# Gate and up of layer 1 by seven block products instead of eight

## The chip, the cores and the metric
The kernel runs on one core of one Trainium2 chip. The metric is the device time of one execution in microseconds (us), the median of several runs. The engines are TensorE (PE; its weight loads are PEld), VectorE (DVE), ScalarE (ACT), GpSimd (POOL) and SyncE (SP), whose queue issues the DMAs.

## The reference
A decoder trunk of two layers on 512 tokens of 1024 features, all in float32. Each layer is a mixer (attention) and a SwiGLU feed-forward block, each behind a modulated RMSNorm; the hidden width is 2816. Cut to what matters here:

```python
D_MODEL = 1024
SEQ = 512
DEPTH = 2
FFN_HIDDEN = ((8 * D_MODEL // 3 + 255) // 256) * 256

def _swiglu(h, wg, wu, wd):
    return (jax.nn.silu(h @ wg) * (h @ wu)) @ wd

def reference(x, c, ...):
    cond = jax.nn.silu(c)
    for l in range(DEPTH):
        mod = cond @ ada_w[l] + ada_b[l]
        sh1, sc1, g1, sh2, sc2, g2 = [m[:, None, :] for m in jnp.split(mod, 6, axis=-1)]
        h = _rms_norm(x, norm_mix[l]) * (1.0 + sc1) + sh1
        ...
        x = x + g1 * (y @ w_out[l])
        h = _rms_norm(x, norm_ffn[l]) * (1.0 + sc2) + sh2
        x = x + g2 * _swiglu(h, ffn_gate[l], ffn_up[l], ffn_down[l])
    return x
```

## The kernel before
**Arithmetic.** Activations lie feature-major: x is eight tiles (k-tiles) of 128 features by 512 tokens. A float32 product is made of three products of rounded operands: every operand is split into hi (a copy rounded to float32r, on ScalarE) and lo (the operand less hi, on VectorE), and `mm3` (line 438) issues hi x hi, hi x lo and lo x hi, each a matmul with a weight load of its own. `mms` (line 422) issues them all on line 431.

**Weights.** `stream` (line 519) lists units of 128 partitions x 2048 columns, one DMA of 1 MB each on SP, into `raw` (three slots). `prep_to` (line 546) splits a unit in four pieces of 512: four copies (`whi`, on ScalarE, `copy`/`act`, line 457) and four subtractions (`wlo`, `tt`, line 473, on VectorE; in an early part of layer 0 the second half of a unit on GpSimd). `whi` and `wlo` have three slots each, and a slot comes free when the whole unit has been used. `unit` (line 561) hands out the next unit and records the splits of those ahead.

**Gate and up.** Each layer has 22 tiles f of 128 hidden features. One unit `wg` holds the gate and the up weights of one f: 2 x 8 blocks of 128 x 128, the gate's in the first 1024 columns. `ffn_tile` (line 1100) makes 8 k-tiles x 2 results x 3 = 48 matmuls of 512 tokens into two PSUM banks, then Silu (ScalarE), the product (VectorE), a rounded copy (ScalarE) and the remainder (VectorE) into `hid`. The first two f run in two halves of 256 tokens (96 matmuls of 256 columns each), so that they can begin when the norm of the first half is done. `ffn` (line 1113) does f = 0 to 10, then a down product over these (`reduce_out`, line 1071), then f = 11 to 21 and the last down product.

**Order.** Nothing runs in the order of the text. Each operation is recorded with an estimated duration (`mm_ns`, `ve_ns`, the sums in `act`) and with the tiles it touches; a list scheduler (`once`, line 240) then simulates the engines, lets each take the ready operation of the smallest number first (VectorE's are renumbered by when TensorE would want the result, `due`, line 216), gives out the slots of `raw`, `whi`, `wlo`, `t2` (61 tiles of 512 columns: activations, `hid`, temporaries), `sm` and `ps` (eight PSUM banks), and writes a fixed order for each engine. The waits between engines follow from the tiles. A tag can have a cap (`gu`, the banks of gate and up: 4), and t2 keeps 8 tiles for whoever is next in the recorded order.

Names in the trace: `t` is any t2 tile, `ps` a PSUM bank, `raw`, `whi`, `wlo` the weights, `x` the residual.

Of the kernel before, what the change touches and what calls it, by code (L numbers as in the profile page):

```python
# [17 lines left out]
P = 128  # L18
# [7 lines left out]
BIG = 1e30  # L26
TOPK = 128
# [50 lines left out]
class View:  # L78
# [32 lines left out]
    def region(self):  # L111
        """bits of the (32-partition quadrant, column block) pairs touched, and elements per partition"""
# [46 lines left out]
class Sched:  # L159
    CROSS, SAME, DMA = 270, 130, 2300  # L160
    # the PE's clock is halved at first and for a while after a long gap
# [54 lines left out]
    def due(self):  # L216
        """priorities from when the PE, kept busy in the present order, would want each result"""
# [151 lines left out]
class Kern:  # L369
    def __init__(self, ctx, tc, io, out):  # L370
# [887 lines left out]
```

## Time and profile before
| | us |
|---|---|
| median of 3 runs (1207.24 to 1208.63) | 1207.81 |
| span of the profiled execution | 1205.3 |
| TensorE busy | 1180.9 |
| VectorE busy | 707.4 |
| ScalarE busy | 487.1 |
| GpSimd busy | 87.9 |

The span goes from the first to the last instruction of one execution; the runs' median is 2.5 us above it. A busy time is a sum over the whole span and says nothing of which engine sets the time in one stage; for that, look at a stretch alone. The mixer of layer 0 (with its output product) runs to some 300 us, its feed-forward block to some 665, the mixer of layer 1 to some 840; the gate and up tiles of layer 1 from f = 3 on lie from 873 to 960 and from 1020 to 1140 us, each group followed by its down product.

### The profile page before, as it was taken

The page shows a single profiled execution, that of the slowest core. Times are in us where ns is not written, and L with a number is a line of the kernel's source. Part 1 is how long each engine was busy: PE and PEld are TensorE (multiplying, and loading weights), DVE is VectorE, ACT ScalarE, POOL GpSimd, SP SyncE. Part 2 cuts the span into 40 slices and gives each one's busy share as a digit, 9 for nine tenths or more (in the row PEclk, how much of TensorE's full clock was granted, in tenths as well). Part 3 has the DMA queues.
Part 4 walks back from the last instruction along what each step waited for, and adds up shares of the span by engine and source line. Part 5 has one row for each costly group of instructions (what it writes and reads, how often), then busy time and mean ns, then how long its engine had stood idle before and what let it go on. Part 6 is the DMA issues. An engine that isn't in the chain of part 4 may idle for free.

```text
span 1205.3 us, 16639 instructions
## 1 busy us (share of the span) xinstructions
PE 1180.9 (98%) x6424; PEld 956.2 (79%) x6424; DVE 707.4 (59%) x1656; ACT 487.1 (40%) x1194; POOL 87.9 (7%) x224
## 2 busy tenths in 40 slices
PE   6989999999999999999999999999999999999998
PEld 3867667679988888888889876669988888888888
DVE  5599999847875456655443967748633323233321
ACT  5464376755433221232232666755423312223310
POOL 0142332300000000000000120100000000000000
PEclk9999999999999999999999999999999999999999
DMA  9545612202585546655511322011422223322211
GB/s 349 228 140 175 245 41 101 76 31 71 179 299 185 175 155 216 226 189 175 175 59 65 105 71 71 1 71 70 141 105 77 98 88 105 105 105 95 80 53 36
DMA packets 32415, 151.58 MB, mean 126 GB/s; under 512 B 3152, under 2 KB 4304, under 8 KB 21072
## 3 DMA queue, kind: packets, MB, share of 16 engines
q1 hardware_dynamic: 32336, 150.52, 35.6%
q8 instruction: 50, 0.82, 0.3%
q14 instruction: 29, 0.24, 0.1%
HBM read 148.41 MB, written 2.10 MB: 125 GB/s over the span
## 4 chain that ended last, share of the span: by engine, by line
PE 89%; DVE 7%; ACT 2%; issue 1%; POOL 0%; DMA 0%; SPq 0%; DVEq 0%; POOLq 0%; ACTq 0%
PE ps L431 86%; PE ps L442 3%; DVE t L488 2%; ACT t L457 1%; DVE wlo L473 1%; DVE sm L857 1%; DVE t L858 1%; DVE t L473 1%; DVE t L493 1%; DVE t L481 1%; DMA x<-in_x 0%; POOL sm L473 0%; DVE sm L499 0%; ACT whi L457 0%; ACT sm L457 0%
## 5 line engine op out<-in xcount | busy, mean ns | idle before, releaser
L431 PE MATMUL ps<-t,whi 128*128 128x512 f32 (+2 forms) x2864 | 774.7, 358 | 0.9 <-ACT t L457 0.9
L431 PEld LDWEIGHTS ps<-t,whi 128*128 128x128 f32 x2864 | 506.7, 189 | 82.8 <-issue 4.5
L431 PE MATMUL ps<-t,wlo 128*128 128x512 f32 (+2 forms) x1432 | 509.9, 356 | 0.0
L431 PEld LDWEIGHTS ps<-t,wlo 128*128 128x128 f32 x1432 | 270.6, 189 | 38.1
L457 ACT ACTIVATE t<-ps 128x512 f32<-128x512 f32 (+6 forms) x274 | 120.3, 475 | 399.5 <-PE ps L431 372.2
L457 ACT ACTIVATE whi<-raw 128x512 fp32r<-128x512 f32 x364 | 206.8, 621 | 163.3 <-PE ps L431 98.9
L473 DVE TENSOR_TENSOR wlo<-raw,whi 128x512 fp32r<-128x512 f32 x340 | 221.8, 691 | 38.7 <-ACT whi L457 38.3
L473 DVE TENSOR_TENSOR t<-ps,t 128x128 fp32r<-128x128 f32 (+4 forms) x120 | 56.2, 489 | 220.5 <-PE ps L431 202.1
L431 PE MATMUL ps<-whi,t 128*128 128x512 f32 (+1 forms) x512 | 172.9, 394 | 1.1 <-DVE t L488 1.1
L431 PEld LDWEIGHTS ps<-whi,t 128*128 128x128 f32 x512 | 95.0, 189 | 29.5 <-issue 7.8
L488 DVE SCALAR_TENSOR_TENSOR x<-ps,mod,x 128x512 f32<-128x512 f32 (+1 forms) x64 | 39.3, 616 | 115.2 <-PE ps L431 114.7
L431 PE MATMUL ps<-wlo,t 128*128 128x512 f32 (+1 forms) x256 | 96.5, 377 | 0.0
L488 DVE SCALAR_TENSOR_TENSOR t<-raw,cond,t 128x512 f32<-128x512 f32 x112 | 79.1, 761 | 19.5 <-DMA raw<-in_ada 19.5
L431 PE MATMUL ps<-t,t 64*128 64x256 f32 (+5 forms) x592 | 82.8, 347 | 0.2 <-ACT t L457 0.2
L431 PEld LDWEIGHTS ps<-t,t 64*128 64x128 f32 (+2 forms) x592 | 54.3, 181 | 28.4 <-issue 15.1
L457 ACT ACTIVATE t<-t,sm 128x256 f32<-128x256 f32 (+3 forms) x128 | 65.5, 516 | 20.4 <-DVE sm L493 12.6
L442 PE MATMUL ps<-cst,t 128*128 128x128 f32 x388 | 61.8, 279 | 10.0 <-DVE t L473 6.8
L442 PEld LDWEIGHTS ps<-cst,t 128*128 128x128 f32 x388 | 45.0, 140 | 32.6 <-issue 9.9
L481 POOL TENSOR_SCALAR sm<-sm 128x8 f32<-128x8 f32 (+2 forms) x64 | 18.4, 288 | 550.8 <-DVE sm L499 547.4
L473 DVE TENSOR_TENSOR t<-t,t 128x512 fp32r<-128x512 f32 (+3 forms) x85 | 50.2, 593 | 14.1 <-ACT t L457 13.9
L431 PEld LDWEIGHTS ps<-wlo,t 128*128 128x128 f32 x256 | 48.4, 189 | 6.2
L493 DVE CUSTOM_DVE_ANT_0 t<-ps,cst 128x256 f32<-128x256 f32 (+3 forms) x104 | 39.1, 409 | 18.5 <-PE ps L431 18.1
(72 smaller groups left out, 564.6 us busy)
## 6 DMA issues: line engine op xcount, KB each, us to landing
raw<-in_wg SPq DMA_DIRECT2D x44, 1024.0 KB, 4.8
raw<-in_ada SPq DMA_DIRECT2D x40, 1024.0 KB, 5.3
raw<-in_wd SPq DMA_DIRECT2D x20, 1024.0 KB, 4.7
raw<-in_w0c SPq DMA_DIRECT2D x10, 1024.0 KB, 6.1
t<-in_ada SPq DMA_DIRECT2D x32, 256.0 KB, 6.5
raw<-in_wo SPq DMA_DIRECT2D x8, 1024.0 KB, 4.8
raw<-in_w1c SPq DMA_DIRECT2D x6, 1024.0 KB, 4.7
x<-in_x SPq DMA_DIRECT2D x8, 256.0 KB, 5.1
```

The source lines that it names most:

```text
L431: self.nc.tensor.matmul(o.ap(), l.ap(), r.ap(), start=st, stop=sp, skip_group_check=True)
L442: self.s.op("PE", 107, lambda: self.nc.tensor.transpose(out.ap(), src.ap(), self.ident.ap()), [out], [src, self.ident])
L457: self.nc.scalar.activation(out.ap(), src.ap(), func, **kw)
L473: lambda: self.eng(e).tensor_tensor(out.ap(), a.ap(), b.ap(), op=op), [out], [a, b])
L481: self.eng(e).tensor_scalar(out.ap(), a.ap(), val(s1), val(s2), op0=op0, **kw)
L488: lambda: self.nc.vector.scalar_tensor_tensor(out.ap(), a.ap(), val(s), b.ap(), op0=op0, op1=op1),
L493: lambda: self.nc.vector.tensor_tensor_reduce(out.ap(), a.ap(), b.ap(), op0=OP.add, op1=OP.min, scale=scale, scalar=3e38, accum_out=accum. ...
L857: self.s.op("DVE", 65 + 1.05 * n, lambda m8=m8: self.nc.vector.max(m8.ap(), sc.ap()), [m8], [sc])
L858: self.s.op("DVE", 65 + 1.05 * n, lambda m8=m8: self.nc.vector.match_replace(sc.ap(), m8.ap(), sc.ap(), -3e38), [sc], [m8, sc])
```

## The change
In layer 1, from f = 3 on, gate and up of one tile are no longer two results over all eight k-tiles, but a 2 x 2 block product: the blocks of the weights are (gate, up) by (first, last four k-tiles), those of the activations (first, last four k-tiles) by (first, last 256 tokens). It is done with seven block products in place of eight (the scheme of Winograd's variant of Strassen). Each block product is 4 k-tiles x 3 = 12 matmuls of 256 columns, and three PSUM banks are used.

- `prep_seven` makes the weights' operands: it sums blocks of the raw weights (VectorE, over 1024 and 512 columns), and splits seven operands of 512 columns, the pairs at once over 1024.
- `combos` runs once, ahead of f = 3: it adds the shift to the eight kept norm results `hf`, makes four combinations of them for each pair of k-tiles, and splits them.
- `ffn_seven` runs the products, with two copies, an in-place subtraction in PSUM and two more subtractions between and behind them, then Silu, product and split as before.
- The split weights of all units, in both layers, now lie in 13 tiles of 1024 columns (`w`) in place of three `whi` and three `wlo` of 2048; t2 has 59 tiles instead of 61, with a cap of 18 for the tag T; the cap `gu` is 6 instead of 4; the planner's estimate for GpSimd is 2.48 ns an element instead of 2.1. Units that are not taken apart in sevens are split in pieces of 512 as before (the first unit in pieces of at most 512 within halves of 800).

The diff, cut to its core (removed comments and the arguments `e` and `e_`, which no call sets, are left out):

```diff
+NW, NT2 = 13, 59
+SEVEN, DIRECT = (1,), 3
...
-        s.group("whi", pool("whi", 3), 3, 0, None)
-        s.group("wlo", pool("wlo", 3), 3, 0, None)
-        n = 61
-        s.group("t2", pool("t2", n), n, 8, None, L=12, pT=4, qf=3, q=8, nt=10, hid=26, ada0=20)
+        s.group("w", pool("w", NW), NW, 0, None)
+        n = NT2
+        s.group("t2", pool("t2", n), n, 8, None, L=12, pT=4, qf=3, q=8, nt=10, hid=26, ada0=20, T=18)
-        s.group("ps", pool("ps", 8, space=PSUM), 8, 1, None, mm=3, lg=2, tp=2, pv=2, gu=4, st=7)
+        s.group("ps", pool("ps", 8, space=PSUM), 8, 1, None, mm=3, lg=2, tp=2, pv=2, gu=6, st=7)
...
-            return 165 + 2.1 * n
+            return 165 + 2.48 * n
...
+            if self.seven(i):
+                self.prep_seven(i, raw)
+            else:
+                step = 800 if name == "w0s" else 1024
+                for a in range(0, w, step):
+                    m = min(step, w - a)
+                    self.split_w(i, raw[:, a:a + m], m, 512, e if a else "DVE")
...
+    def split_w(self, i, src, n, step, e="DVE"):
+        hi, lo = (self.s.tile("w", "w", (P, 1024), FR)[:, :n] for _ in range(2))
+        for a in range(0, n, step):
+            b = min(a + step, n)
+            self.copy(hi[:, a:b], src[:, a:b])
+            self.tt(lo[:, a:b], src[:, a:b], hi[:, a:b].bitcast(F), OP.subtract, e=e)
+        self.ws[i].append((hi, lo))
+
+    def prep_seven(self, i, raw):
+        q = raw.rearrange("p (q c) -> p q c", q=4)
+        s13 = self.s.tile("w", "w", (P, 1024))
+        s13v = s13.rearrange("p (q c) -> p q c", q=2)
+        two = lambda: [self.s.tile("w", "w", (P, 1024), FR) for _ in range(2)]
+        halves = lambda t: [t[:, a:a + 512] for a in (0, 512)]
+        self.tt(s13v, q[:, 0::3], q[:, 2][:, None].to_broadcast([P, 2, 512]), OP.add)
+        xh, xl = two()
+        self.copy(xh, raw[:, :1024])
+        self.tt(xl, raw[:, :1024], xh.bitcast(F), OP.subtract)
+        self.tt(q[:, 2], s13[:, 512:], q[:, 0], OP.add)
+        sh, sl = two()
+        self.copy(sh, s13)
+        self.tt(sl, s13, sh.bitcast(F), OP.subtract)
+        self.tt(q[:, 1], q[:, 2], q[:, 1], OP.add)
+        th, tl = two()
+        for a in (512, 0):
+            c = slice(a, a + 512)
+            r = raw[:, 512 + a:1024 + a]
+            self.copy(th[:, c], r)
+            self.tt(tl[:, c], r, th[:, c].bitcast(F), OP.subtract)
+        y = self.s.tile("w", "w", (P, 1024), FR)
+        self.copy(y[:, :512], q[:, 3])
+        self.tt(y[:, 512:], q[:, 3], y[:, :512].bitcast(F), OP.subtract)
+        X, S, T = (list(zip(halves(h), halves(l))) for h, l in ((xh, xl), (sh, sl), (th, tl)))
+        self.ws[i] = [X[0], T[1], S[1], X[1], S[0], T[0], tuple(halves(y))]
...
+    def combos(self):
+        c1, c2 = HALVES
+        T = []
+        for k in range(8):
+            t = self.hf[k]
+            self.act(t, t, AF.Identity, bias=self.mod[1][:, 3, k:k + 1])
+        for k in range(4):
+            f, g = self.hf[k], self.hf[k + 4]
+            p, q = self.t2("T"), self.t2("T")
+            self.tt(p[:, c1], f[:, c1], f[:, c2], OP.subtract)
+            self.tt(p[:, c2], g[:, c2], p[:, c1], OP.add)
+            self.tt(q[:, c1], f[:, c2], g[:, c2], OP.subtract)
+            self.tt(q[:, c2], g[:, c1], p[:, c2], OP.subtract)
+            o = []
+            for t in (p, q):
+                hi, lo = self.t2("h", dt=FR), self.t2("h", dt=FR)
+                self.copy(hi, t)
+                self.tt(lo, t, hi.bitcast(F), OP.subtract)
+                o += [(hi[:, c], lo[:, c]) for c in HALVES]
+            T.append(o)
+        return T
+
+    def ffn_seven(self, H, T, w, hid):
+        c1, c2 = HALVES
+        a, b, e = (self.ps("gu")[:, c1] for _ in range(3))
+        B11 = [tuple(t[:, c1] for t in H[k]) for k in range(4)]
+        B21 = [tuple(t[:, c1] for t in H[k]) for k in range(4, 8)]
+        B22 = [tuple(t[:, c2] for t in H[k]) for k in range(4, 8)]
+        T1, T2, T3, T4 = ([T[k][j] for k in range(4)] for j in range(4))
+
+        def product(out, j, B, start=False):
+            for k in range(4):
+                wh, wl = (t[:, k * P:(k + 1) * P] for t in w[j])
+                self.mm3(out, wh, wl, B[k][0], B[k][1], start and k == 0, k == 3)
+        pq, u, sg = (self.t2("sg") for _ in range(3))
+        product(a, 0, B11, True)
+        self.copy(pq[:, c1], a)
+        product(b, 1, T2, True)
+        self.tt(b, b, pq[:, c1], OP.subtract)
+        self.copy(u[:, c1], b)
+        product(e, 2, T1, True)
+        self.copy(pq[:, c2], e)
+        product(a, 3, B21)
+        self.act(sg[:, c1], a, AF.Silu, after=self.lnexp)
+        product(b, 4, T3)
+        self.tt(u[:, c2], b, pq[:, c2], OP.subtract)
+        product(e, 5, B22)
+        self.tt(sg[:, c2], e, u[:, c1], OP.subtract)
+        self.act(sg[:, c2], sg[:, c2], AF.Silu)
+        product(b, 6, T4)
+        self.tt(sg[:, c1], b, sg[:, c1], OP.mult)
+        self.tt(sg[:, c2], u[:, c2], sg[:, c2], OP.mult)
+        self.copy(hid[0], sg)
+        self.tt(hid[1], sg, hid[0].bitcast(F), OP.subtract)
+        return sg
...
-                sg = self.ffn_tile(H, f, c, w(f), hid[f - a])
+                if l not in SEVEN or f < DIRECT:
+                    sg = self.ffn_tile(H, f, c, w(f), hid[f - a])
+                else:
+                    T = T or self.combos()
+                    sg = self.ffn_seven(H, T, w(f), hid[f - a])
```

`norm_tile` keeps its temporary for the second norm of layer 1 in eight T tiles (`hf`) instead of the tag nt. The seven products are called P0 to P6 below, in the order of `ffn_seven`. No load of weights changes.

## Rows read from the trace of the kernel before

**Rows 1.** Page, part 1: the span; busy time, share and instructions of each engine
```profile
span 1205.3 us, 16639 instructions
...
PE 1180.9 (98%) x6424; PEld 956.2 (79%) x6424; DVE 707.4 (59%) x1656; ACT 487.1 (40%) x1194; POOL 87.9 (7%) x224
```

**Rows 2.** Page, part 4: the chain that ended last, shares by engine
```profile
PE 89%; DVE 7%; ACT 2%; issue 1%; POOL 0%; DMA 0%; SPq 0%; DVEq 0%; POOLq 0%; ACTq 0%
```

**Rows 3.** Stretches: length, busy us (instructions) per engine, granted clock, DMA share, GB/s
```profile
core 0: us, PE busy (x) PEld busy (x) DVE busy (x) ACT busy (x) POOL busy (x), PEclk, DMA share, GB/s
30.00:240.00 210.00, 200.40 (x1239) 147.97 (x1241) 187.15 (x499) 119.94 (x343) 61.58 (x142) 1.00 0.40 144
60.00:240.00 180.00, 170.64 (x1011) 123.15 (x1011) 170.83 (x459) 106.72 (x298) 58.10 (x135) 1.00 0.37 129
855.80:873.00 17.20, 17.20 (x106) 15.43 (x105) 7.19 (x15) 6.15 (x14) 0.00 (x0) 1.00 0.54 184
873.00:960.00 87.00, 87.00 (x385) 72.07 (x384) 29.58 (x48) 25.74 (x48) 0.00 (x0) 1.00 0.28 97
1020.00:1140.00 120.00, 120.00 (x532) 99.37 (x531) 40.12 (x65) 34.65 (x65) 0.00 (x0) 1.00 0.30 104
```

**Rows 4.** What TensorE's matmuls waited for, whole span: total us, times, longest
```profile
PE ps L431 <- DVE t L473: 6.9, 2, 6.4
PE ps L442 <- DVE t L473: 6.8, 8, 2.4
```

**Rows 5.** Timeline of TensorE in a whole gate-up tile: start us, us, what
```profile
873.65 0.62 PE L431 MATMUL ps<-t,whi 128*128 128x512 f32 x2
874.10 0.39 PE L431 MATMUL ps<-t,wlo 128*128 128x512 f32 x1
874.33 0.62 PE L431 MATMUL ps<-t,whi 128*128 128x512 f32 x2
```

**Rows 6.** Timeline of TensorE, a half tile with 256 columns
```profile
846.90 0.40 PE L431 MATMUL ps<-t,whi 128*128 128x256 f32 x2
847.14 0.28 PE L431 MATMUL ps<-t,wlo 128*128 128x256 f32 x1
847.26 0.40 PE L431 MATMUL ps<-t,whi 128*128 128x256 f32 x2
```

**Rows 7.** Timeline of ScalarE: Silu of three whole tiles, and one pair of copies
```profile
873.16 0.60 ACT L457 ACTIVATE t<-ps 128x512 f32<-128x512 f32 x1 [7.81 <-PE ps L431]
873.66 1.15 ACT L457 ACTIVATE whi<-raw 128x512 fp32r<-128x512 f32 x2
...
1030.92 0.60 ACT L457 ACTIVATE t<-ps 128x512 f32<-128x512 f32 x1 [8.23 <-PE ps L431]
...
1139.72 0.60 ACT L457 ACTIVATE t<-ps 128x512 f32<-128x512 f32 x1 [7.66 <-PE ps L431]
```

**Rows 8.** Timeline of VectorE: two products of halves, one whole product, one split pair
```profile
855.06 0.75 DVE L473 TENSOR_TENSOR t<-ps,t 128x256 f32<-128x256 f32 x2
...
873.91 0.69 DVE L473 TENSOR_TENSOR t<-ps,t 128x512 f32<-128x512 f32 x1 [7.57 <-PE ps L431]
874.52 1.28 DVE L473 TENSOR_TENSOR wlo<-raw,whi 128x512 fp32r<-128x512 f32 x2
```

**Rows 9.** Groups by line and shape: x, busy us, mean ns, idle before
```profile
L473 DVE TENSOR_TENSOR wlo<-raw,whi 128x512 fp32r<-128x512 f32 x112 | 71.4, 683 | 18.8 <-ACT whi L457 18.8
...
L473 DVE TENSOR_TENSOR t<-ps,t 128x256 f32<-128x256 f32 x8 | 3.1, 418 | 3.9 <-ACT t L457 3.9
```

**Rows 10.** Timeline around 804 us: a ScalarE copy that VectorE's subtraction waits for
```profile
804.05 1.25 ACT L457 ACTIVATE t<-ps 128x128 fp32r<-128x128 f32 x3 [0.36 <-DVE t L473]
804.36 0.69 DVE L473 TENSOR_TENSOR t<-ps,t 128x128 fp32r<-128x128 f32 x3 [0.34 <-ACT t L457]
```

**Rows 11.** Groups of VectorE by line and shape, 855.8 to 873 us
```profile
L473 DVE TENSOR_TENSOR wlo<-raw,whi 128x512 fp32r<-128x512 f32 x8 | 5.1, 687 | 0.1
```

More of the change, by code (lines that the diff above doesn't have):

```diff
@@ L550, in prep_to @@
             w = self.units[i][2]
+            name, idx, _ = self.units[i]
             raw = self.raws.pop(i)
-            hi = self.s.tile("whi", "whi", (P, 2048), FR)
-            lo = self.s.tile("wlo", "wlo", (P, 2048), FR)
-            for a in range(0, w, 512):
-                b = min(a + 512, w)
-                self.copy(hi[:, a:b], raw[:, a:b])
-                self.tt(lo[:, a:b], raw[:, a:b], hi[:, a:b].bitcast(F), OP.subtract, e="POOL" if a >= 1024 and 2 < i < 15 else "DVE")
-            self.ws[i] = (hi, lo)
@@ L559, in prep_to, with seven @@
-            self.prepped += 1
+            self.ws[i] = []
+            e = "POOL" if 2 < i < 15 else "DVE"
+            if self.seven(i):
[5 more added lines that the diff above has]
+                    self.split_w(i, raw[:, a:a + m], m, 512, e if a else "DVE")
+            self.prepped += 1
+    def seven(self, i):
+        name, idx, _ = self.units[i]
+        return name[:2] == "wg" and int(name[2]) in SEVEN and idx >= DIRECT
@@ L568, in chunk @@
     def chunk(self):
-        ua, ub = self.unit(), self.unit(2)
-        a, b = ([t.rearrange("p (k c) -> p k c", k=4) for t in u] for u in (ua, ub))
-        return lambda k: (a[0][:, k], a[1][:, k]) if k < 4 else (b[0][:, k - 4], b[1][:, k - 4])
+        ts = self.unit() + self.unit(2)
+        return lambda k: tuple(t[:, (k % 2) * 512:(k % 2) * 512 + 512] for t in ts[k // 2])
     def setup(self):
@@ L645, in mod_first, with mod_rest @@
         self.stt(self.G[0][0][:, k:k + 1], self.mod[0][:, 1, k:k + 1], 1.0, self.ng[:, 0, 0, k:k + 1], OP.add, OP.mult)
-    def mod_rest(self, l, v, on_pe):
+    def mod_rest(self, l, v, on_pe, e_="DVE"):
         ps = acc = None
@@ L723, in norm_tile @@
         sh = self.mod[l][:, 3 * n, k:k + 1]
-        t = self.t2("nt")[:, c]
+        if n == 1 and l in SEVEN:
+            if c.start == 0:
+                if k == 0:
+                    self.hf = []
+                self.hf.append(self.t2("T"))
+            t = self.hf[k][:, c]
+        else:
+            t = self.t2("nt")[:, c]
         hi, lo = H[k][0][:, c], H[k][1][:, c]
@@ L951, in even @@
         self.score, self.iw, self.bv = {}, {}, {}
-        hi, lo = self.unit()
-        hi, lo = (t[:, :1600].rearrange("p (k c) -> p k c", k=8) for t in (hi, lo))
-        small = [self.proj_f(H, i, lambda k: (hi[:, k], lo[:, k]), 200, "st") for i in range(NB)]
+        ws = self.unit()
+        w0s = lambda k: tuple(t[:, (k % 4) * 200:(k % 4) * 200 + 200] for t in ws[k // 4])
+        small = [self.proj_f(H, i, w0s, 200, "st") for i in range(NB)]
         w = self.chunk()
@@ L1077, in block @@
             while len(blocks) <= j:
-                hi, lo = self.unit()
+                u = self.unit()
                 w = self.units[self.cursor - 1][2]
-                blocks.extend((hi[:, a:a + P], lo[:, a:a + P]) for a in range(0, w, P))
+                blocks.extend(tuple(t[:, a % 1024:a % 1024 + P] for t in u[a // 1024]) for a in range(0, w, P))
             return blocks[j]
@@ L1104, in ffn_tile @@
             for s in range(2):
-                self.mm3(ps[s][:, c], hi[:, s, k], lo[:, s, k], H[k][0][:, c], H[k][1][:, c], k == 0, k == KT - 1)
+                a = s * 1024 + k * P
+                wh, wl = (t[:, a % 1024:a % 1024 + P] for t in w[a // 1024])
+                self.mm3(ps[s][:, c], wh, wl, H[k][0][:, c], H[k][1][:, c], k == 0, k == KT - 1)
         sg = self.t2("sg")[:, c]
@@ L1119, in w @@
                 if f not in W:
-                    W[f] = [t.rearrange("p (s k c) -> p s k c", s=2, k=8) for t in self.unit()]
+                    W[f] = self.unit()
                 return W[f]
```

13 lines of the change are left out of this document (7 added, 6 removed).

## The prediction
> **What bounds the kernel now.** I read the page's totals first: of a span of 1205.3 us TensorE is busy 1180.9 us (98%), VectorE 707.4 us, ScalarE 487.1 us, GpSimd 87.9 us [rows 1]. A busy TensorE could still be waiting for someone's result, so the chain that ended last comes next: 89% of it lies on TensorE, 7% on VectorE [rows 2]. Shares over the whole span hide stages with other limits, so the third view is the table of stretches [rows 3]. From 60 to 240 us (layer 0's mixer) VectorE is busy 170.8 of 180 us and TensorE 170.6: two engines near their limit. From 873 to 960 us and from 1020 to 1140 us (gate and up of layer 1, from the fourth tile on) TensorE is busy all of the time at a granted clock of 1.00 (the 2.4 GHz level), VectorE 29.6 of 87 and 40.1 of 120 us, ScalarE 25.7 and 34.7. The change is made in these two stretches: only TensorE's work sets their length, and both other engines have two thirds of their time free. Last the waits: the matmuls waited for VectorE 13.7 us in the two largest groups, the longest single wait being 6.4 us [rows 4], none of it in these stretches, where busy time equals length.
>
> **TensorE's part.** A tile's gate and up is now 2 results x 8 k-tiles x 3 products of hi and lo = 48 matmuls of 512 columns. Three of them take 874.33 - 873.65 = 0.68 us from start to start [rows 5], so one takes 0.2267 us and a tile 10.88 us. Counted another way, the Silu at 1030.92 and the one ten tiles later at 1139.72 are 108.80 us apart: 10.88 us again [rows 7]. After the change a tile is 7 products x 4 k-tiles x 3 = 84 matmuls of 256 columns. These exist in the trace, in the half tiles of the first two f: three take 847.26 - 846.90 = 0.36 us [rows 6], 0.120 us each. That is 6.7 ns more than half of 0.2267, and it eats much of the eighth that the seven products save: 84 x 0.120 = 10.08 us. The gain is 0.80 us a tile, and with 19 tiles (f = 3 to 21) 15.2 us, all on the path, for as long as TensorE stays the bound.
>
> The Trainium skill has a rule on this (TensorE: Matmul & The Clock Gate, "Back-to-back issue gap"): at the warm clock a matmul starts N/2.4 + 2.5 ns after the last. By it the two sizes would cost 109.2 and 215.8 ns, an estimate from that page, and the tile would save 1.19 us, 22.5 us in all. The rows stand 11 ns above it at both sizes, and I take the rows.
>
> **VectorE's part in the steady tile.** Here the time could be given back. Back to back, 512 columns cost 874.52 - 873.91 = 0.60 us, and 256 columns, second of a pair that takes 0.75 us with a first of 0.42 us, 0.33 us [rows 8, 9]. So each further 256 cost 0.27 us, and 1024 columns, which the trace does not have, some 1.14 us. prep_seven issues three subtractions or sums of 1024 (s13, xl, sl) and five of 512 (two sums, th's two remainders, y's remainder): 3 x 1.14 + 5 x 0.60 = 6.42 us. ffn_seven issues five of 256 and one of 512 behind the products: 5 x 0.33 + 0.60 = 2.25 us. Together 8.67 us a tile, where now six of 512 make 3.6 us. That is 86% of the new 10.08 us: TensorE stays the bound, but the cover shrinks from 7.3 us to 1.4 us a tile.
>
> What that leaves exposed is bounded from both sides. Below by 0: the order is written out ahead, w holds 13 tiles (7 of the running f, five or six of the next), and P0, P2 and P3 of a tile or P0 of the next can stand where an answer is awaited. Above by the nearest rows for a handover: VectorE idles 0.34 us from a ScalarE copy's start to its own subtraction [rows 10]; five uncovered handovers a tile (xl, sl, th twice, y) would bring it to 8.67 + 1.70 = 10.37 us, 0.29 us over, 5.5 us in all. The new in-place subtraction b - pq makes TensorE wait before the fifth product, with P2 and P3 (2.88 us) between; behind the waiting matmul stand all later ones, but the path (two handovers of 0.34 us, 0.33 us on VectorE, a copy of at most 0.60 us on ScalarE, at most one operation of 1.14 us in front) is 2.75 us. I take 0.1 us a tile, 1.9 us, nearer to 0 because other splits are ready at most handovers.
>
> **ScalarE's part.** Two copies of 1024, three of 512 (a pair of 512 takes 1.15 us [rows 7], so at most 2 x 1.15 + 3 x 0.60 = 4.1 us), three copies and two Silus of 256 and one copy of 512, at most 6 x 0.60 = 3.6 us: 7.7 us, under 10.08. It costs nothing while TensorE and VectorE are slower.
>
> **The start.** combos runs once, between the last norm tiles and the second product of f = 3. VectorE gets 16 operations of 256 and eight of 512: 16 x 0.33 + 8 x 0.60 = 10.1 us; ScalarE 8 Identity and 8 copies, some 10 us. The cover is the stretch from 855.8 to 873 us: 17.2 us in which VectorE works 7.2 us and ScalarE 6.2 us [rows 3]. Of VectorE's, eight splits of two units are 4.8 us [rows 11], in whose place f = 3's 6.42 us comes. So 7.2 - 4.8 + 6.4 + 10.1 = 18.9 us against 17.2: 1.7 us late, which I take. The bounds: 0, as half of the combinations (q) is needed only four products later and P0 and P3 need none; and all of VectorE's 10.1 us plus the eight Identity before it at 0.60, some 15 us, if none of it is covered.
>
> **The rest.** Layer 0 issues the same operations; its weights lie in 13 tiles of 1024 in place of six of 2048, so half a unit comes free earlier, t2 has two slots fewer, gate and up may take six PSUM banks for four, and the planner prices GpSimd at 2.48 ns an element for 2.1. All of this only shifts the written order. In the mixer TensorE idles 210 - 200.4 = 9.6 us after 30 us [rows 3]: no more can be won there, and I let it lose no more than that either; I take 0, and 3 us to each side for the range. DMA issues are the same loads in the same order on SP, and raw still has three slots.
>
> **The sum.** Against the profiled span: 1205.3 - 15.2 + 1.9 + 1.7 = 1193.7 us. The runs' median, 1207.8, lies 2.5 us above that span (what lies around it), so 1196.2 us.
>
> **The rivals.**
> *VectorE takes over, mildly.* Its tile comes to between 10.37 and 10.88 us by handovers and work queued in the wrong order; at 10.6 us the gain is 0.28 x 19 = 5.3 us, less 1.7 at the start: 1204.2. For it: 86% use before any wait. Against: in 60 to 240 us VectorE keeps up 95%.
> *VectorE takes over in full, and the kernel gets slower.* If the new operations, each fed by ScalarE or the one before, do not overlap at their ends, they cost their whole durations, 0.683 us for 512 and 0.418 us for 256 [rows 9], 1.21 us for 1024 by the same step: 3 x 1.21 + 6 x 0.683 + 5 x 0.418 = 9.82 us, and with 1.70 us of handovers 11.5 us a tile. From 10.88 us on the change loses; at 11.5 it loses 0.64 x 19 = 12.2 us and 1.7: 1221.7. Against: six operations a tile, alternately fed by ScalarE, already run 0.60 us apart. This case agrees with a rule of the Trainium skill (VectorE: DVE Perf Modes, "The DRAIN you can't avoid"): the next operation does not start until the pipe is empty. Here it starts 0.08 us before the recorded end.
> *The start is bare.* Up to 15 us of combinations in front of f = 3 cancel the gain: 1207.8 - 15.2 + 1.9 + 13 = 1207.5. Against: P0 and P3, and 10 us free on VectorE ahead of it.
> *The shorter matmul costs only its columns.* With 0.2267 / 2 = 0.1133 us each, a tile is 9.52 us, the gain 25.8 us and the time 1185.6. Against: the 0.120 us of [rows 6] is the same shape in the same kernel, back to back. The rule of TensorE: Matmul & The Clock Gate (the Trainium skill, "Back-to-back issue gap") lies between, at an estimated 1188.9 us by its figures.
> *The written order falls otherwise.* The mixer's 9.6 us move by half, in either direction: 1191.4 or 1201.
>
> **How the numbers follow.** About 0.2% (2.4 us) is what a measurement of this kernel can tell from no change, so faster means under 1205.4 and slower over 1210.2. The forecast has 0.60 (1192 to 1201), the mild takeover 0.12, the full one 0.06, the bare start 0.05, columns alone 0.03, the order 0.07 to each side. Faster: 0.60 + 0.10 + 0.03 + 0.07 + 0.05 = 0.85; same: 0.05 + 0.02 + 0.01 = 0.08; slower: 0.06 + 0.01 = 0.07. The range reaches from 1189 (order gained, both losses at 0) to 1205 (the mild takeover), and leaves out columns alone, the bare start, the full takeover and parts of two others, about 0.18.
>
> **What would show it.** Right: three 256-column matmuls in 0.36 us in the new tiles; tiles 10.1 to 10.3 us apart; VectorE 8 to 9 us busy in each; 1024 columns at about 1.2 us recorded; no TensorE wait over 2 us near the first new tile; the stretch up to the first gate-up tile of layer 1 as long as before, within 3 us. Wrong: a VectorE busy over 95% from f = 3 on with TensorE waiting for it, tiles of 10.6 us or more, a gap of many us ahead of f = 3, or a shift in the mixers larger than the gain.

## The result and the profile after

The median of the changed kernel is 1195.61 us (four executions, 1194.65 to 1198.33), that of the kernel before, on the same chip, 1208.03 us (1207.24 to 1208.63). The ratio is 0.9899, with a 95% interval of 0.9887 to 0.9911: faster by 1.0%. The forecast was 1196.2 us, with a range of 1189 to 1205; it lies 0.6 us above the measured time. The profiled execution has a span of 1194.3 us, 11.0 us less than before; by the medians the gain is 12.4 us. The two differ as executions of one kernel do: the profile of before is of one with a mean granted clock of 1.000, as 6 of the 32 executions of that kernel beside the experiments had (median span 1204.8 us), while the other 26 had 0.997 (1206.2 us) and the changed kernel's four 0.994 to 0.996.

First the page: its totals, and the shares of the chain that ended last.

```profile
span 1194.3 us, 18348 instructions
...
PE 1170.6 (98%) x7108; PEld 979.6 (82%) x7108; DVE 817.6 (68%) x1832; ACT 554.9 (46%) x1305; POOL 84.3 (7%) x224
...
PE 86%; DVE 5%; ACT 1%; POOL 0%; issue 0%
```

Against [rows 1] and [rows 2]: TensorE has more instructions (7108 for 6424) and is busy 10.3 us less; VectorE gained 110.2 us, ScalarE 67.8. TensorE still holds 86% of the chain. These sums don't say where the 11 us lie; the stretches of the changed kernel do. The first is what 855.8 to 873 us was before (up to the Silu of f = 2), the second and third are the new tiles of both halves, the fourth is five tiles.

```profile
core 0: us, PE busy (x) PEld busy (x) DVE busy (x) ACT busy (x) POOL busy (x), PEclk, DMA share, GB/s
859.80:877.00 17.20, 17.20 (x106) 15.42 (x105) 16.06 (x32) 11.08 (x19) 0.00 (x0) 1.00 0.19 62
877.00:958.00 81.00, 81.00 (x668) 80.62 (x667) 72.41 (x117) 50.61 (x97) 0.00 (x0) 1.00 0.34 118
1018.00:1120.00 102.00, 102.00 (x849) 101.81 (x848) 87.12 (x135) 61.36 (x112) 0.00 (x0) 1.00 0.27 94
1050.00:1100.40 50.40, 50.40 (x423) 50.40 (x422) 43.89 (x70) 30.43 (x56) 0.00 (x0) 1.00 0.29 104
```

Where [rows 3] had VectorE at 29.6 of 87 us and 40.1 of 120, it now has 72.41 of 81 and 87.12 of 102, yet TensorE is busy all of the time at a clock of 1.00. In the fourth row five tiles take 43.89 us of VectorE: 8.78 us a tile, with 70 instructions, the 14 that `prep_seven` and `ffn_seven` issue for each. The timeline of VectorE in the changed kernel (start, us, what) gives the length of a tile: the same subtraction, which waits for ScalarE's copy, stands at 1082.17 and 1092.25, 10.08 us apart.

```profile
1082.17 0.43 DVE L475 TENSOR_TENSOR ps<-ps,t 128x256 f32<-128x256 f32 x1 [0.45 <-ACT w L459]
...
1086.37 1.22 DVE L475 TENSOR_TENSOR w<-w 128x1024 fp32r<-128x1024 f32 x1
1087.51 0.68 DVE L475 TENSOR_TENSOR w<-raw,w 128x512 fp32r<-128x512 f32 x1
...
1092.25 0.43 DVE L475 TENSOR_TENSOR ps<-ps,t 128x256 f32<-128x256 f32 x1 [0.45 <-ACT w L459]
```

Its second and third line show what 1024 columns cost: 1087.51 - 1086.37 = 1.14 us to the next start, 1.22 us recorded. The matmuls of the new tiles, as the group of TensorE from 1018 to 1120 us (times, busy us, mean ns):

```profile
L433 PE MATMUL ps<-t,w 128*128 128x256 f32 x847 | 102.0, 283 | 0.0
```

With 84 of them in a tile of 10.08 us it is 0.1200 us from one matmul to the next (the 102.0 us hold two matmuls of 512 columns beside the 847; the mean of 283 ns is that of one from end to end, in a pipeline).

To split the span I use two marks on ScalarE: the Silu of the first whole gate-up tile of layer 0, and that of f = 2 in layer 1, the last before the new tiles. In the changed kernel the second reads:

```profile
877.19 0.60 ACT L459 ACTIVATE t<-ps 128x512 f32<-128x512 f32 x1 [3.45 <-PE ps L433]
```

| | before | after |
|---|---|---|
| Silu of the first whole tile, layer 0 | 330.97 | 333.31 |
| Silu of f = 2, layer 1 | 873.16 [rows 7] | 877.19 |
| from there to the end of the span | 332.1 | 317.1 |

So the new tiles and all behind them are 15.0 us shorter, and what lies ahead of them is 4.0 us longer: 2.3 us up to the first mark, 1.7 us between the marks. 15.0 - 4.0 = 11.0. The gain is where it was forecast; the 4.0 us come from a part of the program in which no arithmetic operation was changed but the combinations and the first weights of f = 3, which came in just ahead of the second mark (without them it is 3.7 us, run 1). What TensorE's matmuls waited for (total us, times, longest) hardly differs from [rows 4]. The one matmul that waits for a remainder of weights is not in the new tiles but at the start of layer 0:

```profile
PE ps L433 <- DVE t L475: 7.1, 3, 6.6
PE ps L444 <- DVE t L475: 7.0, 8, 2.5
...
PE ps L433 <- DVE w L475: 0.4, 1, 0.4
```

```profile
23.57 0.44 PE L433 MATMUL ps<-t,w 128*128 128x384 f32 x1 [0.39 <-DVE w L475]
```

### The profile page after: what moved, and what is told of

Its sections match the earlier page's. It is cut to its first block, busy times and chain, and to the rows that moved or that the text cites. A ratio compares the mean times of both kernels' runs of the same rounds, so it can differ in the third digit from the quotient of the medians.

```text
span 1194.3 us, 18348 instructions
## 1 busy us (share of the span) xinstructions
PE 1170.6 (98%) x7108; PEld 979.6 (82%) x7108; DVE 817.6 (68%) x1832; ACT 554.9 (46%) x1305; POOL 84.3 (7%) x224
## 4 chain that ended last, share of the span: by engine, by line
PE 86%; DVE 5%; ACT 1%; POOL 0%; issue 0%
PE ps L433 82%; PE ps L444 3%; DVE t L910 1%; DVE t L490 1%; DVE sm L909 1%; DVE w L475 1%; ACT t L459 0%; DVE t L475 0%; DVE t L495 0%; POOL sm L475 0%; DVE sm L501 0%; DVE t L483 0%; ACT sm L459 0%; POOL sm L483 0%; DVE sm L490 0%
## 5 line engine op out<-in xcount | busy, mean ns | idle before, releaser
L433 PE MATMUL ps<-t,w 128*128 128x256 f32 (+2 forms) x4980 | 833.7, 328 | 0.9 <-DVE w L475 0.4
L433 PEld LDWEIGHTS ps<-t,w 128*128 128x128 f32 x4980 | 735.4, 190 | 86.0 <-issue 5.3
L475 DVE TENSOR_TENSOR w<-raw,w 128x512 fp32r<-128x512 f32 (+1 forms) x340 | 235.4, 726 | 136.3 <-PE ps L433 105.2
L459 ACT ACTIVATE w<-raw 128x512 fp32r<-128x512 f32 (+1 forms) x364 | 217.1, 645 | 153.8 <-PE ps L433 126.4
L459 ACT ACTIVATE t<-ps 128x256 f32<-128x256 f32 (+6 forms) x331 | 137.9, 447 | 289.7 <-PE ps L433 235.7
L433 PE MATMUL ps<-w,t 128*128 128x512 f32 (+1 forms) x768 | 189.9, 391 | 1.3 <-DVE t L490 1.3
L433 PEld LDWEIGHTS ps<-w,t 128*128 128x128 f32 x768 | 133.6, 190 | 36.7 <-issue 9.3
L490 DVE SCALAR_TENSOR_TENSOR t<-raw,cond,t 128x512 f32<-128x512 f32 x112 | 77.3, 746 | 17.3 <-DMA raw<-in_ada 17.2
L475 DVE TENSOR_TENSOR t<-t,t 128x256 f32<-128x256 f32 (+3 forms) x124 | 66.7, 555 | 20.4 <-ACT t L459 20.2
L475 DVE TENSOR_TENSOR t<-ps,t 128x256 f32<-128x256 f32 (+4 forms) x158 | 66.1, 440 | 19.0 <-ACT t L459 12.7
L459 ACT ACTIVATE t<-t 128x256 f32<-128x256 f32 (+3 forms) x82 | 43.8, 540 | 27.8 <-DVE t L475 27.1
```

The source lines that it names most:

```text
L433: self.nc.tensor.matmul(o.ap(), l.ap(), r.ap(), start=st, stop=sp, skip_group_check=True)
L459: self.nc.scalar.activation(out.ap(), src.ap(), func, **kw)
L475: lambda: self.eng(e).tensor_tensor(out.ap(), a.ap(), b.ap(), op=op), [out], [a, b])
L490: lambda: self.eng(e).scalar_tensor_tensor(out.ap(), a.ap(), val(s), b.ap(), op0=op0, op1=op1),
```

## The experiments

**1. The change without the seven products.** All the rest is kept: 13 tiles of 1024, 59 t2 slots, the bank cap, GpSimd's price (only `hf` goes with the products).

```diff
-SEVEN, DIRECT = (1,), 3
+SEVEN, DIRECT = (), 3
```

> The changed kernel with no tile by seven products; its storage, caps and planner figures stay, and the written order of the mixers is that of the changed kernel. Theory (the seven products give 15.2 us, and some 4 us are lost ahead of them by the new storage and order): 1195.6 + 15.2 = 1210.8 us, 3 us over the kernel before, with the first gate-up tile of layer 1 as late as in the changed kernel. Rival (the seven products give only 11 to 12 us, the delay belongs to them): 1207 to 1208 us.

Measured: 1210.87 us, ratio to before 1.0031 [1.0019, 1.0043]; the marks at 332.70 and 876.84, the tail 332.1 us as before. The seven products alone are worth 1210.87 - 1195.61 = 15.3 us (by the two ratios 0.0132 x 1208 = 15.9). The changes around them cost 3.7 us ahead of f = 3 by the marks, and 0.0031 x 1208 = 3.7 us by the ratio. Up to 841 us each engine has the same instructions in the same order in this trace as in the changed kernel's.

**2. The same tiles with small matmuls only.** From f = 3 on every tile of layer 1 runs in two halves of 256 columns, 96 matmuls without a sum of weights.

```diff
-            if self.seven(i):
+            if False:
...
-                    T = T or self.combos()
-                    sg = self.ffn_seven(H, T, w(f), hid[f - a])
+                    for c in HALVES:
+                        sg = self.ffn_tile(H, f, c, w(f), hid[f - a])
```

> Layer 1's tiles from f = 3 on with eight products in halves of 256 tokens: 96 matmuls of 256 columns a tile, no weight sums, no combinations. Theory (0.120 us a matmul in this stage whatever it belongs to): 11.52 us a tile, 19 x 1.44 = 27.4 us over the changed kernel, 1223.0 us. Rival (a matmul of 256 columns costs half of one of 512, the seven products save an eighth and lose the rest elsewhere): 10.88 us a tile, 1210.8 us.

Measured: 1222.8 us, ratio 1.0129 [1.0115, 1.0142]. On ScalarE's timeline the same half's Silu returns every 11.52 us (1040.70, 1052.22, 1063.74):

```profile
1040.70 0.39 ACT L459 ACTIVATE t<-ps 128x256 f32<-128x256 f32 x1 [4.45 <-PE ps L433]
...
1052.22 0.39 ACT L459 ACTIVATE t<-ps 128x256 f32<-128x256 f32 x1 [4.45 <-PE ps L433]
...
1063.74 0.39 ACT L459 ACTIVATE t<-ps 128x256 f32<-128x256 f32 x1 [4.45 <-PE ps L433]
```

11.52 / 96 = 0.1200 us a matmul, with VectorE's work as small as before. The 0.120 us is the price of the shape, not of waits for VectorE: the rival "columns only" falls by this, and so does any thought that a faster VectorE would shorten the seven products.

**3. One more operation of 1024 on VectorE in each tile.** The sum s13 is made twice, with the same result.

```diff
         self.tt(s13v, q[:, 0::3], q[:, 2][:, None].to_broadcast([P, 2, 512]), OP.add)
+        self.tt(s13v, q[:, 0::3], q[:, 2][:, None].to_broadcast([P, 2, 512]), OP.add)
```

> The first sum over 1024 columns (s13) is made twice for each of the 19 tiles, with the same result: 1.14 us more of VectorE a tile, on the way to the weights. Theory (VectorE works 8.8 us of a tile's 10.08 us, its 1024 columns cost 1.14 us back to back, and the order lets it run ahead): 9.9 us a tile still fit, 1195.6 us, at most 0.2 us a tile (4 us) more. Rival (operations fed by another engine do not overlap, VectorE is at its limit already): 1.14 us x 19 = 22 us more, 1213 to 1217 us.

Measured: 1201.49 us, ratio 0.995 [0.9936, 0.9963]: 5.9 us over the changed kernel, more than the 4 us that my theory allowed and less than the rival's. The tail is 323.6 us, 6.5 more. By busy time alone nothing should be lost: 8.78 + 1.14 = 9.92 us, under 10.08. Three stretches of this kernel show how it is lost all the same:

```profile
1030.00:1110.00 80.00, 80.00 (x669) 80.00 (x668) 75.06 (x110) 46.35 (x86) 0.00 (x0) 1.00 0.30 106
884.00:900.00 16.00, 12.88 (x102) 12.07 (x101) 15.45 (x25) 8.36 (x18) 0.00 (x0) 1.00 0.18 67
1110.00:1130.00 20.00, 18.03 (x148) 17.63 (x147) 19.01 (x34) 12.06 (x26) 0.00 (x0) 1.00 0.26 91
```

From 1030 to 1110 us TensorE is full, as it is in the changed kernel. But 80 us are 7.94 tiles of 10.08 us, 119 VectorE operations at 15 a tile, and VectorE did 110: it falls behind by 8%. The groups of VectorE in these 80 us show with what:

```profile
L475 DVE TENSOR_TENSOR w<-raw 128x1024 f32<-128x1024 f32 x16 | 19.5, 1220 | 0.4 <-PE ps L433 0.2
...
L475 DVE TENSOR_TENSOR t<-ps,t 128x256 f32<-128x256 f32 x21 | 8.5, 419 | 1.1 <-ACT t L459 0.6 <-PE ps L433 0.6
...
L475 DVE TENSOR_TENSOR t<-t,t 128x512 fp32r<-128x512 f32 x4 | 2.7, 685 | 0.0
```

The sums of the weights keep up (16, two for each of eight tiles). What is put off is the end of the tiles' own work: 21 operations from PSUM for 24 in the same stretch of the changed kernel, and 4 remainders of `hid` for 7. That holds TensorE up only later. It loses time behind the start (3.1 us of the 16 from 884 us on) and late in the second group (2.0 of the 20 from 1110), and there it waits for operations on t tiles, of ScalarE and VectorE, not for weights. The timeline of TensorE there (the wait before a start in brackets):

```profile
1121.14 1.70 PE L433 MATMUL ps<-t,w 128*128 128x256 f32 x12 [1.72 <-DVE t L475]
```

The waits of both stretches are 5.1 of the 6.5 us; the rest is not placed. 6.5 us over 19 tiles is 0.34 us a tile: of the 1.14 us added, 0.8 us were taken up. VectorE itself stood idle 4.9 of the 80 us, 0.62 us a tile, though it was behind. So handovers of about this size do exist; in the changed kernel they lie in the 10.08 - 8.78 = 1.3 us that VectorE has left.

**4. Two more.** s13 and xl are both made twice.

```diff
+        self.tt(s13v, q[:, 0::3], q[:, 2][:, None].to_broadcast([P, 2, 512]), OP.add)
...
-        self.tt(xl, raw[:, :1024], xh.bitcast(F), OP.subtract)
+        for _ in range(2):
+            self.tt(xl, raw[:, :1024], xh.bitcast(F), OP.subtract)
```

> The sum s13 and the remainder xl, both over 1024 columns, are made twice: 2.28 us more of VectorE a tile. Theory: 8.8 + 2.3 = 11.1 us a tile, 1.0 us over TensorE's 10.08; VectorE takes over in both groups of tiles, less what it made ahead before the second group: 0.9 to 1.0 us x 19 = 17 to 19 us more, 1212 to 1215 us. Rival (VectorE has more room than its busy time tells): 1196 to 1200 us.

Measured: 1219.49 us, ratio 1.0104 [1.0087, 1.0122], 23.9 us over the changed kernel and past what was expected. The profiled execution was the longest of the four, 1223.41 us, with a span 26.6 us over the changed kernel's: 3.8 us of it lie ahead of f = 3 (the mark stands at 881.00), 22.8 us behind. The 3.8 us are no work of the new tiles: with this edit VectorE's order already differs from 126 us on, in the first mixer. By work alone VectorE's tile is 8.78 + 2 x 1.14 = 11.06 us, 0.98 over TensorE's, 18.6 us in 19 tiles. VectorE is now the bound, busy 76.05 of 78 and 96.78 of 100 us:

```profile
880.00:958.00 78.00, 69.47 (x543) 67.30 (x542) 76.05 (x114) 39.73 (x77) 0.00 (x0) 0.98 0.24 83
1040.00:1140.00 100.00, 93.79 (x748) 92.48 (x747) 96.78 (x141) 54.35 (x100) 0.00 (x0) 0.97 0.27 95
```

TensorE idles 8.5 and 6.2 us here, and its granted clock has come down to 0.98 and 0.97: where it waits again and again, it also works more slowly, by an estimated 0.02 x 78 + 0.03 x 100 = 4.6 us. This is the full takeover of the prediction, and 2.28 us of added work a tile are enough for it.

**5. The 1024 columns in halves.** s13, xl and sl, and the copies that feed them, by 512.

```diff
-        self.tt(xl, raw[:, :1024], xh.bitcast(F), OP.subtract)
+        for c in (slice(0, 512), slice(512, 1024)):
+            self.copy(xh[:, c], raw[:, c])
+            self.tt(xl[:, c], raw[:, c], xh[:, c].bitcast(F), OP.subtract)
```

(the same for s13 with sh and sl)

> The weight operands of the seven products by operations of 512 columns only: s13, xl, sl and the two copies in two halves each. Theory (a wide operation saves 2 x 0.60 - 1.14 = 0.06 us on VectorE and less than 0.1 us on ScalarE): 0.2 us a tile, 9.0 of 10.08 us, hidden: 1195 to 1197 us. Rival (VectorE has no room left at the ends of the two groups, as when s13 is made twice): 2 to 5 us more, 1198 to 1201 us.

Measured: 1196.81 us, ratio 0.9905 [0.9891, 0.992], not to be told from the changed kernel by the time; the trace has a tail of 318.2 us, 1.1 us longer, with a wait of 0.5 us near 890 us. The longer operations are not what the gain hangs on: three times 2 x 0.60 - 1.14 = 0.06 us a tile is little.

**6. One direct tile less ahead of the combinations.** f = 2 goes by seven products too.

```diff
-SEVEN, DIRECT = (1,), 3
+SEVEN, DIRECT = (1,), 2
```

> The seven products from f = 2 on: one more such tile (-0.8 us), but the combinations lose the cover of one direct tile of 10.9 us. Theory (that cover hid the start): VectorE ends the combinations some 9 us after TensorE could use them, P0 and P3 hide 2.9 us of it, so TensorE waits some 6 us ahead of the first new tile: 1195.6 - 0.8 + 6 = 1201 us (1199 to 1204). Rival (the start costs nothing anywhere, VectorE catches up): 1194.8 us.

Measured: 1201.55 us, ratio 0.9959 [0.9944, 0.9974]: one more tile by seven, and 5.9 us slower, as the theory had it. But the waits for it are smaller than its 6 us. TensorE's timeline shows what the direct f = 2 had covered, waits of 0.85 and 2.38 us in brackets:

```profile
875.21 6.03 PE L433 MATMUL ps<-t,w 128*128 128x256 f32 x48 [0.85 <-ACT t L459]
883.61 2.78 PE L433 MATMUL ps<-t,w 128*128 128x256 f32 x15 [2.38 <-DVE t L475]
```

and VectorE's, in the same kernel, why: remainders of the combinations stand at 876 to 879 us, while TensorE is in the first of the new tiles already.

```profile
876.32 1.28 DVE L475 TENSOR_TENSOR t<-t,t 128x512 fp32r<-128x512 f32 x2
...
878.12 1.29 DVE L475 TENSOR_TENSOR t<-t,t 128x512 fp32r<-128x512 f32 x2
```

The two waits are 3.2 of the 6.7 us (5.9 and the 0.8 of the tile). Another part is the granted clock, which falls behind the second wait:

```profile
885.00:890.00 5.00, 5.00 (x32) 4.96 (x32) 5.00 (x14) 3.14 (x8) 0.00 (x0) 0.70 0.57 210
```

**7. GpSimd's price put back.** In the changed kernel, 2.1 ns an element, as before.

```diff
-            return 165 + 2.48 * n
+            return 165 + 2.1 * n
```

> The changed kernel with the planner's old estimate for GpSimd (2.1 ns an element). Theory (the delay ahead of the feed-forward blocks comes from the planner's estimate, which moves the order of the mixer): the third gate-up tile of layer 1 ends as in the kernel before, 4 us sooner, 1191.6 us. Rival (it comes from the weights' 13 tiles of 1024 and the two t2 tiles fewer): 1195 to 1197 us.

Measured: 1201.07 us, ratio 0.995 [0.9937, 0.9962]. Neither theory held: the 4.0 us do not come back, 4.7 us more are lost by the second mark (5.5 by the medians). The marks stand at 337.93 and 881.91, the tail is 317.4 us: 4.6 of the 4.7 us lie ahead of the first mark.

**8. The price alone, in the kernel before.**

```diff
-            return 165 + 2.1 * n
+            return 165 + 2.48 * n
```

> The kernel before with one figure of the planner changed: 2.48 ns an element for GpSimd in place of 2.1. No operation, no size is changed, only the written order. Theory (any figure that moves the order of layer 0's mixer loses the few us by which the order of before is a good one): 1209 to 1212 us, all of the difference before the first gate-up tile of layer 1. Rival (the delay needs the new storage of the weights): 1206.5 to 1208.5 us.

Measured: 1209.5 us, ratio 1.0013 [1.0004, 1.0021]; the marks at 332.35 and 874.54, 1.4 us later, the tail unchanged at 332.1. VectorE's order differs from that of before from some 60 us on. The mean clock of the profiled execution is 0.997, and its span of 1206.6 us is within 0.4 of the median of before's executions at 0.997 (1206.2).

**9. The smaller t2 alone, in the kernel before.**

```diff
-        n = 61
+        n = 59
```

> The kernel before with 59 tiles of t2 in place of 61. Theory (as with the planner's figure: only the written order moves): 1209 to 1212 us. Rival (t2 is not what held the mixer): 1206.5 to 1208.5 us.

Measured: 1214.29 us, ratio 1.0051 [1.0035, 1.0066], more than expected; the marks at 336.84 and 879.01, 5.9 us later, the tail 332.1 us.

**10. Another price in the changed kernel.**

```diff
-            return 165 + 2.48 * n
+            return 165 + 2.6 * n
```

> The changed kernel with 2.6 ns an element for GpSimd in the planner. Theory (such a figure only draws another written order for the mixers; the feed-forward block of layer 1 takes what it took): 1191 to 1202 us, with the third gate-up tile of layer 1 ending between 873 and 882 us and the time behind it 317 us as in the changed kernel. Rival (the figure itself matters, the higher the later): over 1200 us with the mixers alone later by over 5 us.

Measured: 1196.6 us, ratio 0.9903 [0.9888, 0.9918]; marks at 333.48 and 877.36, tail 317.3.

Runs 7 to 10 belong together. The tail takes 332.1 us in each version without the seven products and 317.1 to 317.4 in each with them. The part ahead varies:

| | mark in layer 0 | mark in layer 1 | between |
|---|---|---|---|
| before | 330.97 | 873.16 | 542.2 |
| before, price 2.48 | 332.35 | 874.54 | 542.2 |
| before, 59 t2 slots | 336.84 | 879.01 | 542.2 |
| changed, without the seven products | 332.70 | 876.84 | 544.1 |
| changed, price 2.1 | 337.93 | 881.91 | 544.0 |
| changed | 333.31 | 877.19 | 543.9 |
| changed, price 2.6 | 333.48 | 877.36 | 543.9 |

None is as early as the kernel before. Each mark is that of one execution: in the four traces that have the changed kernel's instructions in its order up to 841 us (its own and those of runs 1, 3 and 5) the first mark lies from 332.27 to 333.31, so a difference of 1 us there need not be the order's. The smaller t2 on its own costs some 5.9 us ahead of the first mark, the price on its own 1.4 us, little more than that spread, and with the new tiles of the weights a price of 2.48 makes 4.6 us good that 2.1 loses. These effects don't add up: there one written order is changed for another. Between the marks it is otherwise: neither the price nor the t2 slots change anything there, and every version with the new tiles of the weights and the bank cap takes 1.7 to 2.0 us longer.

**11. The seven products in layer 0 as well,** from f = 11 on, where the combinations have the first down product as cover. In the first half of the block four steps of the background work (the next modulation vectors) go with each tile instead of two, so that VectorE is free of them by then.

```diff
-SEVEN, DIRECT = (1,), 3
+SEVEN, DIRECT = (0, 1), (11, 3)
...
-                self.run_bg(2)
+                self.run_bg(4 if pi == 0 else 2)
```

(`combos` and `DIRECT` go by layer)

> Seven products also in layer 0, for its tiles f = 11 to 21, with the modulation vectors computed beside f = 0 to 10 at twice the rate, so that VectorE is free of them later. Theory (0.80 us a tile wherever VectorE has 8.8 us free): 1195.6 - 11 x 0.80 = 1186.8 us. Rival (VectorE or the slots of the raw weights are short where the modulation is made, or the start of the combinations is bare): 1191 to 1200 us.

Measured: 1186.87 us, ratio 0.9826 [0.9809, 0.9842], the fastest of all: 8.7 us under the changed kernel, where 11 tiles x 0.80 = 8.8 us were to be had. The stretches of layer 0 show why nothing is given back: TensorE is full while VectorE has 25 to 26 of 30 us in the new tiles, and 22.80 of 30 while it does the background work ahead of them.

```profile
440.00:470.00 30.00, 30.00 (x139) 24.38 (x137) 22.80 (x36) 6.44 (x10) 0.00 (x0) 1.00 0.61 210
500.00:530.00 30.00, 30.00 (x252) 30.00 (x251) 26.40 (x44) 18.85 (x34) 0.00 (x0) 1.00 0.34 125
530.00:560.00 30.00, 30.00 (x252) 30.00 (x251) 25.23 (x40) 17.42 (x33) 0.00 (x0) 1.00 0.23 83
560.00:590.00 30.00, 30.00 (x251) 29.85 (x250) 25.89 (x43) 18.84 (x37) 0.00 (x0) 1.00 0.31 107
```

## Why the prediction was right, and where it was not

**TensorE's part: right.** 15.2 us were forecast; the tail shrank by 15.0 us, and run 1 and the changed kernel are 15.3 us apart. 0.1200 us a matmul for the 0.120 of [rows 6], and 10.08 us a tile for 10.08. The formula of the Trainium skill (TensorE: Matmul & The Clock Gate, "Back-to-back issue gap") that the prediction puts beside this is given there for an isolated matmul; of a stream of weight loads and matmuls, which this is, the section says that both set the spacing, about 131 ns at 512 columns. Neither is borne out here, with 120.0 ns at 256 columns and 226.7 ns at 512. The measurement decides.

**VectorE's part in the steady tile: work right, loss oversized.** 8.67 us a tile were worked out, 8.78 measured; 1.14 us for 1024 columns, exactly as estimated, with a record of 1.22 for the forecast 1.21. (874.52 - 873.91 is 0.61 us, not the 0.60 of the prediction; that moves the sum by under 0.1 us.) The next operation starts 0.08 us ahead of the recorded end of the one before, as in the kernel before. The rule of the Trainium skill (VectorE: DVE Perf Modes, "The DRAIN you can't avoid"), that it does not start until the pipe is empty, is neither borne out nor refuted by this, as no row shows when the pipe is empty; that this case agrees was too much to say. The loss of 1.9 us did not come: TensorE was full in the 81 and the 102 us of the new tiles. The reason given for taking it small, work that is ready ahead, fits this, and runs 3 and 4 show its limit: with 1.14 us more a tile VectorE puts work off until TensorE waits for it, and 0.34 us a tile are lost; with 2.28 us more VectorE is the bound outright. Of the 1.4 us of cover that I counted, 1.3 were there by busy time, and some 0.8 could be used (1.14 - 0.34, run 3).

**ScalarE's part: right.** 50.61 of 81 and 61.36 of 102 us busy, 6.1 us for each of the five tiles in the fourth row above (30.43 / 5), under the 7.7 allowed.

**The start: mechanism right, term oversized.** 1.7 us were allowed, none can be found: VectorE worked 16.06 of the 17.20 us in front of the Silu of f = 2, for the 18.9 of my sum, and TensorE all of them. The last remainders of the combinations (t from t and t) begin at 872.98 and are over by 875.5, ahead of that Silu; what follows is weights' work again:

```profile
872.98 2.49 DVE L475 TENSOR_TENSOR t<-t,t 128x512 fp32r<-128x512 f32 x4
875.39 1.29 DVE L475 TENSOR_TENSOR w<-raw,w 128x512 fp32r<-128x512 f32 x2
876.96 1.23 DVE L475 TENSOR_TENSOR w<-w 128x1024 fp32r<-128x1024 f32 x1 [0.28 <-PE ps L433]
```

My sum put all of the splits of f = 3 into these 17.2 us. Run 6 confirms the cover: take f = 2 away from it, and the change loses 5.9 us, and 3.2 us of waits stand right there.

**The rest: this step failed.** "I take 0", with 3 us to each side for the range; 4.0 us were lost by the profiles, and the sign that I named (the stretch ahead of the new tiles as long as before within 3 us) came out wrong by them: the first Silu of layer 1's gate and up comes at 850.04 for 845.39 us, that of f = 2 4.0 us later. By the medians it is less, 15.0 - 12.4 = 2.6 us, and by the interval of the ratio 1.3 to 4.2. The reason that I gave for a small loss, TensorE's 9.6 us of idle time in the mixer as a cap on either side, is not a reason: idle time caps what can be won, and nothing caps a loss. Run 1 shows that the changes around the seven products are what did it. Of these the slots and the price were tried alone (runs 8 and 9), the 13 tiles and the bank cap were not. I had two rivals for it, 1191.4 and 1201, with 0.07 each; that a planner's changed figures move the order is near certain, and the marks say how far: 1.4 to 8.7 us, in all six versions later.

So the time was right by a sum of errors. 1.9 + 1.7 = 3.6 us of losses were taken in that weren't there, 4.0 us that were there were left out, and 0.2 us of TensorE's gain did not come; 4.0 + 0.2 - 3.6 = 0.6 us is the miss by spans (1194.3 for 1193.7). By the medians the time came out 0.6 us under the forecast, not over it, as the median execution lies nearer to the profiled span here than the 2.5 us of before: that it comes so close is luck.

**What stays open** is by which way the 4.0 us are lost. 1.7 of them lie between the marks, and there in layer 1's mixer and first three gate-up tiles: from the first mark to the end of layer 0's last down product it is 336.6 us in both kernels, and from there to the second mark (before, then after)

```profile
667.57:873.16 205.59, 204.25 (x1228) 161.46 (x1227) 147.21 (x457) 124.84 (x368) 23.18 (x76) 1.00 0.22 78
669.91:877.19 207.28, 204.62 (x1228) 161.20 (x1227) 152.80 (x466) 130.93 (x372) 20.31 (x76) 1.00 0.18 62
```

TensorE idles 2.7 us there for 1.3, at a clock of 1.00. By the table this goes with the new tiles of the weights or the bank cap; which of the two was not tried. The other 2.3 us lie in layer 0 ahead of the first mark, up to 1 us of them within the spread of executions. One place can be seen there. Stretches of 5 us in the first mixer, in the kernel before (busy times of TensorE, its weight loads, VectorE, ScalarE, GpSimd, then the clock):

```profile
140.00:145.00 5.00, 3.96 (x22) 3.14 (x21) 5.00 (x17) 1.40 (x5) 2.89 (x8) 1.00 0.86 323
145.00:150.00 5.00, 5.00 (x33) 3.87 (x33) 4.88 (x14) 1.29 (x5) 1.71 (x6) 1.00 0.58 188
150.00:155.00 5.00, 5.00 (x28) 3.94 (x25) 4.93 (x18) 5.00 (x16) 0.00 (x0) 1.00 0.13 49
```

and in the changed kernel:

```profile
140.00:145.00 5.00, 2.53 (x12) 1.79 (x11) 5.00 (x16) 1.11 (x3) 1.24 (x6) 1.00 0.75 299
145.00:150.00 5.00, 4.18 (x18) 2.83 (x19) 5.00 (x14) 1.06 (x4) 1.94 (x6) 0.59 0.35 110
150.00:155.00 5.00, 5.00 (x25) 3.70 (x22) 4.96 (x18) 5.00 (x15) 0.00 (x0) 0.72 0.25 103
```

TensorE has 12 matmuls instead of 22 in the first of them, and its granted clock then falls to 0.59 and 0.72 while the kernel before holds 1.00. The row of TensorE's timeline in the changed kernel gives the wait ahead of it, for VectorE, of 2.47 us:

```profile
144.86 0.87 PE L444 MATMUL ps<-cst,t 128*128 128x128 f32 x6 [2.47 <-DVE t L475]
```

VectorE is busy all of these first 5 us in both kernels; in the changed one it has other work in front of what TensorE waits for. That would be a wait and a slower clock after it. But run 8, the kernel before with the other price, has the same in the same place, and more of it:

```profile
140.00:145.00 5.00, 1.76 (x8) 1.13 (x6) 5.00 (x17) 1.00 (x3) 1.58 (x6) 1.00 0.68 250
145.00:150.00 5.00, 3.95 (x16) 3.32 (x18) 4.96 (x13) 0.99 (x3) 1.64 (x6) 0.53 0.24 64
```

and its first mark is 1.4 us later than before, not 2.3. Most executions of the kernel before, with their mean clock of 0.997, will have had some such fall as well, though no trace of one was kept. Nor does the delay go with the clock: in run 7 the mean clock of the whole span is 0.997, as against 0.996 in the changed kernel and 1.000 before, and it lost 8.7 us ahead of f = 3 for 4.0. How much of the 2.3 us is the execution, the clock and the order of VectorE's work, I can't separate; no version was run with the order of the one and the storage of the other.

## What to carry to other kernels

Price a shortened matmul by a measured one of the same shape, since the constant part of each eats into what fewer columns save: here 0.80 us a tile instead of the 1.36 of an eighth. Where work is moved to an engine that has room, find the room by adding an operation until it hurts, as the busy share hides the handovers and the lead that buffers give: here 13% of free time (1.3 us a tile) took up 0.8 of the 1.14 us of one more operation. And with an order that is written by a scheduler, any changed size or price moves stages that the change doesn't touch: allow several us for that, mostly as a loss if the present order is a good one, and read those stages by marks of their own, from more than one execution: here one and the same order put its mark 1 us apart.

## What the hardware showed that I had not expected

The matmuls here have a fixed part: 226.7 ns at 512 columns [rows 5] and 120.0 at 256 give 213.4 ns for 512 columns' worth of work and 13.3 ns over, for each one. Two sizes always allow such a line; a third bears it out. In layer 0 of the kernel before three matmuls of 384 columns take 0.52 us, 173 ns each, where 160.0 + 13.3 make 173.3:

```profile
52.55 0.51 PE L431 MATMUL ps<-t,whi 128*128 128x384 f32 x2
...
53.07 0.51 PE L431 MATMUL ps<-t,whi 128*128 128x384 f32 x2
```

At 200 columns it no longer holds: three take 0.34 us (from 53.68 to 54.02), 113 ns each for the 97 of the line.

Some of VectorE's remainder pairs of 512 in the first mixer take twice as long as the 1.28 us of [rows 8]; the timeline of VectorE in the changed kernel has

```profile
64.67 2.67 DVE L475 TENSOR_TENSOR w<-raw,w 128x512 fp32r<-128x512 f32 x2
...
136.62 2.51 DVE L475 TENSOR_TENSOR w<-raw,w 128x512 fp32r<-128x512 f32 x2
```

both while GpSimd makes remainders of its own. But in the kernel before, a pair beside GpSimd's work (at 137.48 us) took 1.27 us. There it was GpSimd that took longer: its two remainders from 137.61 us on took 3.54 us, where the mean of its 24 is 1.435 each. Why it falls on one or the other was not tried. Last, a wait of 2.47 us among sparse matmuls was followed by a mean clock of 0.59 for 5 us (0.5 is the lower level, 1.2 GHz) and of 0.72 for the next 5, with TensorE busy 4.18 of the first 5 us and all of the second.
